# A hybrid decoder block on one core: gates reloaded for eight V chunks at a time, seven activation slots fewer, and one input load handed from SyncE to GpSimd

## The chip, the cores and the metric

The kernel runs on one core of one Trainium2 chip. The metric is the device time of one launch in microseconds (us). Three runs of the kernel before gave 1536.69, 1538.11 and 1542.17 us; the median is 1538.11 us. Differences of about half a per cent (some 8 us) are what such runs can tell from no change.

## The reference

One layer of a decoder over 512 tokens of 1024 numbers: a mixer (16 SSD heads and 8 latent-attention heads, one output projection), a layer norm, a PEER expert mixer, a layer norm. The change touches only the PEER part:

```
def peer(x, w_query, sub_keys, u_table, v_table):
    def block(xb):                                   # blocks of 128 tokens
        q = (xb @ w_query).reshape(T, 8, 2, 128)
        s = einsum('thkd,hknd->thkn', q, sub_keys)
        ...                                          # top 16 of each half, top 16 of the 256 sums
        gate = softmax(top_s)                        # 8 heads x 16 experts for each token
        u = take(u_table, expert_idx)                # 16384 experts, rows of 1024
        act = gelu(einsum('td,thkd->thk', xb, u))
        v = take(v_table, expert_idx)
        return einsum('thk,thkd->td', gate * act, v)
```

## The kernel before

Tokens 0 to 383 of the PEER part are worked densely and the last 128 sparsely. The dense way multiplies all 16384 experts: the u table stands in 128 chunks of 128 experts (`ut`), each a tile of 128x1024, and so does the v table. A "U chunk" is 24 matmuls of 304 columns (three passes of a split into a high and a low part, written `wih` and `wil`), then Gelu into an activation tile (`act`, `acts`). A "V chunk" multiplies the activations of 128 experts by their gates (`P`), splits the product (`Ph`, `Pl`) and adds 18 matmuls of 512 columns into six accumulators (`va`). Tokens 304 to 383 (80 sets) get their u products row by row instead (`urow`: 80 gathers by GpSimd, each followed by one VectorE product), and tokens 384 to 511 are wholly sparse: 128 gathered u rows and 128 gathered v rows (`row`).

The stages in order of time, in the profiled execution: mixer and norms to about 410 us; queries and top-16 to 528 us; decoding of the indices to about 605 us; the build of the gates from 605 to about 840 us; the V stage from 866 us to the end. U chunks are worked beside queries, decoding and build, 88 of them (`PRE`) ahead of the V stage. In the build, 48 steps each make the gates of eight tokens by one-hot products on VectorE, copies on ScalarE and matmuls on TensorE; finished gates of 32 tokens (a block) are scaled into activations that already exist (`late`, L1332, for the first `done[k]` chunks) and the gates of the other chunks are stored to memory (`gsp`). In the V stage they come back chunk by chunk into `gt`. The first 20 V chunks (`GAP`) go alone, then the last 40 U chunks and V chunks alternate ("pairs"), then V chunks go alone again.

What orders the work: one instruction stream for each engine, written out when the program is built. SyncE's queue issues the loads of `ut` and `v` (L113), each into one of four raw tiles, once the split that read the old content is done. In the build, a running sum of estimated times (`tm`) for TensorE and VectorE decides where the halves of a U chunk are put; whether such a half falls into a stretch marked `beside` decides whether GpSimd (L143, 2.4 us) or VectorE (L145, 1.2 us) makes the low part. The u gathers of the 80 sets run six rows ahead (`UROWS`), each issued when a row is used up.

Activations live in `LEAD = KEEP + MORE + REST` slots (47 + 12 + 8 = 67). U chunks beyond the slots that are open are stored (`asp`) and fetched back by GpSimd (`refill`, L1433) as V chunks free slots; `GAP = PRE - LEAD - 1` follows from it.

At 528 us the input rows of the sets are loaded into unused columns of `XT`: two loads and one by GpSimd (L1538, L1539), and eight of 16 partitions each by SyncE (L1541, tile `UR["xb"]`, pieces of 256 B), for the last 16 sets.

Of the kernel before, what the change touches and what calls it, by code (L numbers as in the profile page):

```python
# [11 lines left out]
F32 = mybir.dt.float32  # L12
# [6 lines left out]
OP = mybir.AluOpType  # L19
# [22 lines left out]
REST = 8  # L42
# [10 lines left out]
GP = 4  # L53
# [18 lines left out]
def tile_block(ctx: ExitStack, tc: tile.TileContext, I, out):  # L72
# [1080 lines left out]
    def ug_dots():  # L1153
# [3 lines left out]
        for n in range(UG):  # L1157
            r = UR.pop(n)
            V.scalar_tensor_tensor(r, r, 1.0, UR["xp"], op0=OP.mult, op1=OP.mult,  # L1159
                                   accum_out=hd[:, n:n + 1] if n < UA else hb[:, n - UA:n - UA + 1])  # L1160
            ug_fetch(n + UROWS)
            if n == 1:
                G.dma_start(UR["ixb"], bass.AP(tensor=ixd.tensor, offset=ixd.offset, ap=[[UB, 128 // UB], [128, UB], [1, UB]]))
            if n == UA + 3:
                w = UR["w"]
                A.activation(hd[UA:], hd[UA:], AF.Gelu)
                nc.scalar.dma_start(w[:UA, UA:], hd[UA:])
                A.activation(w[:UA, :UA], hd[:UA], AF.Gelu)
            yield 1.2
            if n == UA - 1:  # L1170
                for e in range(2):
                    A.activation(wide(UR["xp"][:, e * 512:(e + 1) * 512]), UR["xb"][:, e * 8:(e + 1) * 8], AF.Copy)
                yield 0.1
# [67 lines left out]
    def build_g():  # L1241
# [44 lines left out]
        for n in range(48):  # L1286
# [27 lines left out]
            if g % 4 == 3:  # L1314
                k = n // 4
                if k < ND:
                    done.append(min(FIRST, un[0] // 4 * 4))
# [222 lines left out]
    for i in range(0, 128, UB):  # L1540
        nc.sync.dma_start(UR["xb"][i:i + UB], wide(xsp[2, UA - UB:UA]))  # L1541
# [89 lines left out]
    def load_g(q):  # L1631
        if 2 <= q < 32 and q not in gt:
            gt[q] = vst.tile([128, NT // 32, 4, 32], F32, name="gt", bufs=2)
            nb = open_(q * 4)
# [8 lines left out]
    def step_g():  # L1643
        if more_g:
            q, b0, b1 = more_g.pop(0)
            m = min(b1, b0 + GP)
            nc.sync.dma_start(gt[q][:, b0:m], gsp[b0:m, :, q * 4:q * 4 + 4, :].rearrange("b j i t -> j b i t"))
# [5 lines left out]
    for q in range(2):  # L1653
        load_g(q)
    while more_g:
        step_g()
# [14 lines left out]
    def v_prep(c):  # L1671
        load_g(c // 4)
        if c % 4 == 0:
            load_g(c // 4 + 1)
# [4 lines left out]
        if nb:  # L1679
            V.tensor_tensor(P[:, :nb * 32].rearrange("p (b t) -> p b t", t=32), a[:, :nb * 32].rearrange("p (b t) -> p b t", t=32),  # L1680
                            gt[c // 4][:, :nb, c % 4, :], op=OP.mult)
        if nb < ND:
            A.activation(P[:, nb * 32:NU], a[:, nb * 32:], AF.Copy)
        A.activation(P[:, NU:].rearrange("p (b t) -> p b t", t=32), G0[:, :, c] if c < 8 else gt[c // 4][:, ND:, c % 4, :], AF.Copy)
        if c > 8 and c % 4 == 3:
            gt.pop(c // 4)
# [3 lines left out]
    def v_sb(c, nm):  # L1690
        if c > LASTC:
# [237 lines left out]
```

## Time and profile before

| quantity | value |
|---|---|
| median of 3 runs | 1538.11 us |
| profiled execution | 1536.83 us |
| its span | 1535.1 us |
| TensorE (PE) busy | 1503.5 us, 98% |
| VectorE (DVE) busy | 1352.3 us, 88% |
| ScalarE (ACT) busy | 769.3 us, 50% |
| GpSimd (POOL) busy | 719.3 us, 47% |
| memory traffic over the span | 428.27 MB, 279 GB/s |

The profiled execution lies 1.3 us under the median and 1.7 us over its own span. TensorE's busy share is an average over stages; what matters is where its few idle microseconds lie, what ended them, and where the granted clock falls below full speed (1.00 is 2.4 GHz, 0.50 is 1.2 GHz).

### The profile page before, as it was taken

The numbers are of one execution on the slowest core, as the hardware profiler recorded it, in microseconds if no ns is written. First come the engines' busy times: TensorE is split into PE (matmuls) and PEld (weight loads), VectorE is DVE, ScalarE is ACT, GpSimd is POOL, SyncE is SP. The second block draws the span as 40 slices with busy tenths as digits, with TensorE's granted clock in tenths as the row PEclk, the third lists the DMA queues.
The fourth block names the chain that finished last, engine by engine and source line by source line (L and its number), as shares of the span: only waits on it lengthen the run. The fifth ranks groups of instructions, "written<-read, shape, count | busy, mean of one in ns | idle before, by whom it ended". The sixth has DMA issues, their size and how long they took to land.

```text
span 1535.1 us, 24872 instructions
## 1 busy us (share of the span) xinstructions
PE 1503.5 (98%) x8664; PEld 1317.7 (86%) x8664; DVE 1352.3 (88%) x2672; ACT 769.3 (50%) x1541; POOL 719.3 (47%) x522
## 2 busy tenths in 40 slices
PE   9999999999999989999999999999999999999997
PEld 7787888878888989998898988999998888888886
DVE  8979768745799989999899588999999999999998
ACT  5564477742333445775666554444444344443442
POOL 0010032420144532778762477666657676776530
PEclk9999999999999999999999999999999999999999
DMA  7243122375423576999998999999999999999994
GB/s 259 94 149 104 57 71 60 110 248 164 141 76 90 141 243 196 388 398 392 404 381 296 357 400 388 395 382 404 400 399 398 397 395 385 381 388 383 372 318 151
DMA packets 159118, 428.27 MB, mean 279 GB/s; under 512 B 18056, under 2 KB 59984, under 8 KB 158736
## 3 DMA queue, kind: packets, MB, share of 16 engines
q1 hardware_dynamic: 98336, 211.72, 39.7%
q0 software_dynamic: 55104, 196.65, 33.6%
q10 hardware_dynamic: 5552, 18.31, 3.1%
q8 instruction: 68, 1.11, 0.3%
q14 instruction: 58, 0.48, 0.1%
HBM read 393.37 MB, written 31.08 MB: 277 GB/s over the span
## 4 chain that ended last, share of the span: by engine, by line
PE 64%; DVE 18%; DMA 8%; issue 4%; ACT 3%; POOL 2%; DVEq 0%; ACTq 0%; POOLq 0%; SPq 0%
PE va L1721 9%; PE va L1724 9%; PE va L1720 9%; PE pu L90 6%; PE pu L91 6%; PE pu L92 5%; DMA wir<-ut 3%; PE pa L91 3%; PE pa L92 3%; PE pa L90 3%; DVE wil L145 2%; DMA row<-v,ix 2%; DVE t L1033 1%; PE pw L90 1%; PE pw L92 1%
## 5 line engine op out<-in xcount | busy, mean ns | idle before, releaser
L131 ACT ACTIVATE wih<-wir 128x1024 fp32r<-128x1024 f32 (+2 forms) x269 | 277.2, 1032 | 159.3 <-DMA wir<-ut 54.0
L145 DVE TENSOR_TENSOR wil<-wir,wih 128x1024 fp32r<-128x1024 f32 (+1 forms) x212 | 255.8, 1208 | 54.1 <-ACT wih L131 41.6
L92 PE MATMUL pu<-XT,wil 128*128 128x304 f32 x1000 | 300.8, 301 | 0.0
L1721 PE MATMUL va<-wil,Ph 128*128 128x512 f32 x726 | 283.1, 390 | 2.8 <-DVE wil L145 2.8
L1586 POOL DMA_INDIRECT row<-v,ix x128 | 222.0, 1734 | 97.4 <-DVE ac L1607 76.8
L90 PE MATMUL pu<-XT,wih 128*128 128x304 f32 x824 | 251.3, 305 | 6.6 <-ACT acts L1449 4.9
L91 PE MATMUL pu<-XT,wih 128*128 128x304 f32 x824 | 250.6, 304 | 0.0
L1586 POOL DMA_INDIRECT row<-u,ix x128 | 180.1, 1407 | 132.4 <-DVE row L1601 67.6
L92 PEld LDWEIGHTS pu<-XT,wil 128*128 128x128 f32 x1000 | 189.4, 189 | 0.0
L1720 PE MATMUL va<-wih,Ph 128*128 128x512 f32 x486 | 189.1, 389 | 0.0
L1607 DVE SCALAR_TENSOR_TENSOR ac<-row,hd,ac 128x1024 f32<-128x1024 f32 x128 | 164.1, 1282 | 4.5 <-DMA row<-v,ix 2.9
L1601 DVE SCALAR_TENSOR_TENSOR row<-row,XT 128x1024 f32<-128x1024 f32 x128 | 154.5, 1222 | 15.1 <-DMA row<-u,ix 14.4
L90 PEld LDWEIGHTS pu<-XT,wih 128*128 128x128 f32 x824 | 156.3, 190 | 9.4 <-ACT acts L1449 5.3
L1721 PEld LDWEIGHTS va<-wil,Ph 128*128 128x128 f32 x726 | 136.3, 188 | 31.4 <-DVE wil L145 4.5
L91 PEld LDWEIGHTS pu<-XT,wih 128*128 128x128 f32 x824 | 156.8, 190 | 1.6
L1724 PE MATMUL va<-wih,Pl 128*128 128x512 f32 x486 | 149.9, 390 | 0.4 <-DVE Pl L1711 0.3
L145 POOL TENSOR_TENSOR wil<-wir,wih 128x1024 fp32r<-128x1024 f32 (+3 forms) x37 | 77.9, 2113 | 145.1 <-ACT wih L131 121.4
L1703 ACT ACTIVATE Ph<-P 128x384 fp32r<-128x384 f32 x121 | 63.1, 522 | 156.0 <-DVE P L1680 132.9
L1724 PEld LDWEIGHTS va<-wih,Pl 128*128 128x128 f32 x486 | 91.1, 188 | 20.0 <-DVE Pl L1711 1.3
L1720 PEld LDWEIGHTS va<-wih,Ph 128*128 128x128 f32 x486 | 91.2, 188 | 18.1
L1159 DVE SCALAR_TENSOR_TENSOR urow<-urow,xp 128x1024 f32<-128x1024 f32 x80 | 93.8, 1215 | 4.0 <-DMA urow<-u,uix 1.8
L1150 POOL DMA_INDIRECT urow<-u,uix x64 | 81.9, 1280 | 30.1 <-DVE urow L1159 13.3
(527 smaller groups left out, 3484.8 us busy)
## 6 DMA issues: line engine op xcount, KB each, us to landing
wir<-ut SPq DMA_DIRECT2D x128, 512.0 KB
wir<-v SPq DMA_DIRECT2D x86, 512.0 KB
wirx<-v SPq DMA_DIRECT2D x42, 512.0 KB
gt<-gsp SPq DMA_DIRECT2D x63, 256.0 KB
wir<-wo SPq DMA_DIRECT2D x26, 512.0 KB
gsp<-stg ACTq DMA_DIRECT2D x24, 448.0 KB
wir<-wf SPq DMA_DIRECT2D x18, 512.0 KB
wir<-wqr SPq DMA_DIRECT2D x16, 512.0 KB
```

The source lines that it names most:

```text
L90: T.matmul(ps, lh, rh, start=start, stop=False)
L91: T.matmul(ps, lh, rl, start=False, stop=False)
L92: T.matmul(ps, ll, rh, start=False, stop=stop)
L131: A.activation(h, r, AF.Copy)
L145: self.lo(n).tensor_tensor(l, r, h, op=OP.subtract)
L1159: V.scalar_tensor_tensor(r, r, 1.0, UR["xp"], op0=OP.mult, op1=OP.mult, accum_out=hd[:, n:n + 1] if n < UA else hb[:, n - UA:n - UA + 1])
L1586: G.indirect_dma_start(out=R[s], out_offset=None, in_=I["u"] if s < 128 else I["v"], in_offset=bass.IndirectOffsetOnAxis(ap=ix3[:, s % 128 ...
L1601: V.scalar_tensor_tensor(wide(r), wide(r), 1.0, x3, op0=OP.mult, op1=OP.mult, accum_out=hd[:, s:s + 1])
L1607: V.scalar_tensor_tensor(ac, r, hd[:, s - 128:s - 127], ac, op0=OP.mult, op1=OP.add)
L1720: T.matmul(va[b][e], Ph[b], h[:, cs], start=c == 0, stop=False)
L1721: T.matmul(va[b][e], Ph[b], l[:, cs], start=False, stop=False)
L1724: T.matmul(va[b][e], Pl[b], h[:, cs], start=False, stop=c == 127)
```

## The change

Four things change. The stored gates are reloaded for eight V chunks at a time (`GC = 8`) in pieces of 8 x 32 numbers (1 KB) instead of 4 x 32 (512 B), two blocks to a load instead of four, so a load still has 256 KB; the two `gt` tiles double in size. `REST` goes from 8 to 1, so there are 60 activation slots and `GAP` becomes 27. The eight `xb` loads leave SyncE's queue at 528 us and are issued by GpSimd among the gathers of sets 2 to 9, in the early build. The `done` counts are rounded down to multiples of 8 (32, 32 and eight times 40 instead of 32, 36 and eight times 44), and three of the seven last V chunks (121 to 123) keep their split products in the ordinary tiles instead of freed activation slots.

```
-REST = 8
+REST = 1
...
-GP = 4
+GP = 2
+GC = 8
...
             if n == 1:
                 G.dma_start(UR["ixb"], bass.AP(tensor=ixd.tensor, offset=ixd.offset, ap=[[UB, 128 // UB], [128, UB], [1, UB]]))
+            if 1 < n < 2 + 128 // UB:
+                G.dma_start(UR["xb"][(n - 2) * UB:(n - 1) * UB], wide(xsp[2, UA - UB:UA]))
...
-                    done.append(min(FIRST, un[0] // 4 * 4))
+                    done.append(min(FIRST, un[0]) // GC * GC)
...
-    for i in range(0, 128, UB):
-        nc.sync.dma_start(UR["xb"][i:i + UB], wide(xsp[2, UA - UB:UA]))
...
-        if 2 <= q < 32 and q not in gt:
-            gt[q] = vst.tile([128, NT // 32, 4, 32], F32, name="gt", bufs=2)
-            nb = open_(q * 4)
+        if 0 < q < 128 // GC and q not in gt:
+            gt[q] = vst.tile([128, NT // 32, GC, 32], F32, name="gt", bufs=2)
+            nb = open_(q * GC + GC - 1)
...
-            nc.sync.dma_start(gt[q][:, b0:m], gsp[b0:m, :, q * 4:q * 4 + 4, :].rearrange("b j i t -> j b i t"))
+            nc.sync.dma_start(gt[q][:, b0:m], gsp[b0:m, :, q * GC:q * GC + GC, :].rearrange("b j i t -> j b i t"))
...
-        load_g(c // 4)
-        if c % 4 == 0:
-            load_g(c // 4 + 1)
+        if c % GC == 0:
+            load_g(c // GC + 1)
...
-        if c > LASTC:
+        if c > LASTC + 3:
```

SyncE's queue at the end of the queries (528 us). `wir` are raw weight tiles, `XT` the columns that take the sets' inputs, `iaE` a constant for the decoding. Before:

```order
L113 DMA wir<-wqr 128x1024
L113 DMA wir<-ut 128x1024 x10
L1541 DMA XT<-xsp 16x16x64 x8
L1549 DMA iaE<-ch 128x256
L113 DMA wir<-ut 128x1024 x40
```

and now (line numbers are one to three higher):

```order
L114 DMA wir<-wqr 128x1024
L114 DMA wir<-ut 128x1024 x10
L1550 DMA iaE<-ch 128x256
L114 DMA wir<-ut 128x1024 x40
L1458 DMA asp<-aout 128x320
```

The eight loads are gone from between the tenth and the eleventh `ut` tile; nothing else stands between them but one small load.

VectorE in the build, from the scaling of the fourth finished block on (`urow` are set products, `oj`, `g` the one-hot factors, the MEMSET of one column goes with a low part that GpSimd makes). Before:

```order
L1332 TENSOR_TENSOR acts<-acts,stg 128x44x32
L142 MEMSET wil 128x1
L1159 SCALAR_TENSOR_TENSOR urow,uhd<-urow,xp 128x1024 x2
L1264 TENSOR_TENSOR oj<-iotaE,jT 128x1024
L1270 TENSOR_TENSOR g<-tens,units 128x2048
L142 MEMSET wil 128x1
L1159 SCALAR_TENSOR_TENSOR urow,uhd<-urow,xp 128x1024 x3
L145 TENSOR_TENSOR wil<-wir,wih 128x1024
```

and now:

```order
L1335 TENSOR_TENSOR acts<-acts,stg 128x40x32
L1160 SCALAR_TENSOR_TENSOR urow,uhd<-urow,xp 128x1024 x2
L146 TENSOR_TENSOR wil<-wir,wih 128x1024 x2
L1267 TENSOR_TENSOR oj<-iotaE,jT 128x1024
L1273 TENSOR_TENSOR g<-tens,units 128x2048
L143 MEMSET wil 128x1
L1160 SCALAR_TENSOR_TENSOR urow,uhd<-urow,xp 128x1024 x3
L1267 TENSOR_TENSOR oj<-iotaE,jT 128x1024
```

The scaled block is four chunks smaller, and VectorE makes two low parts in a stretch where it made one and GpSimd two. Over the whole program GpSimd makes 22 low parts instead of 26 at L143, and VectorE four more.

SyncE's queue among the pairs, where all 12 blocks of gates come back. Before:

```order
L1647 DMA gt<-gsp 128x4x128
L113 DMA wirx<-v 128x1024
L113 DMA wir<-ut 128x1024
L1647 DMA gt<-gsp 128x4x128
L113 DMA wir<-v 128x1024
L113 DMA wir<-ut 128x1024
L1647 DMA gt<-gsp 128x4x128
```

and now:

```order
L1648 DMA gt<-gsp 128x2x256
L114 DMA wir<-v 128x1024
L114 DMA wir<-ut 128x1024
L1648 DMA gt<-gsp 128x2x256
L114 DMA wir<-v 128x1024
L114 DMA wirx<-ut 128x1024
L114 DMA wir<-v 128x1024
```

Loads of the same size come at six of eight V chunks instead of three of four; the fourth raw tile (`wirx`) now takes u chunks among the pairs, where it took v chunks.

## Rows read from the trace of the kernel before

**Rows 1.** Stretches: us, busy PE, PEld, DVE, ACT, POOL, PEclk, DMA share, GB/s.
```profile
530.00:560.00 30.00, 25.75 (x175) 25.50 (x175) 27.00 (x35) 14.88 (x28) 4.60 (x6) 0.94 0.76 180
600.00:650.00 50.00, 49.34 (x439) 48.41 (x438) 49.27 (x75) 33.28 (x82) 35.59 (x26) 1.00 0.91 342
...
750.00:800.00 50.00, 47.67 (x386) 45.42 (x385) 47.10 (x77) 34.76 (x86) 36.76 (x24) 0.97 1.03 397
...
1150.00:1200.00 50.00, 49.03 (x273) 43.47 (x272) 48.27 (x57) 21.61 (x42) 37.39 (x23) 1.00 1.04 397
1200.00:1250.00 50.00, 47.87 (x264) 41.92 (x263) 47.77 (x49) 18.67 (x38) 35.91 (x23) 1.00 1.03 399
...
1300.00:1350.00 50.00, 50.00 (x222) 41.39 (x221) 49.32 (x59) 21.01 (x38) 37.38 (x20) 1.00 1.04 380
```

**Rows 2.** Waits between 500 and 560 us: us in total, times, longest.
```profile
ACT wih L131 <- DMA wir<-ut: 5.5, 1, 5.5
...
PE pu L90 <- ACT acts L1449: 4.3, 1, 4.3
```

**Rows 3.** SyncE's queue in order of time, 505 to 620 us: start, us.
```profile
527.94 5.20 SPq L1541 DMA_DIRECT2D XT<-xsp  x8
...
536.12 83.22 SPq L113 DMA_DIRECT2D wir<-ut  x25
```

**Rows 4.** Chain that ended last, 522 to 560 us: start, us, what.
```profile
536.12 6.64 DMA wir<-ut
...
542.84 1.06 ACT wih L131
```

**Rows 5.** Busy time around the wait of rows 2; columns as in rows 1.
```profile
541.00:546.00 5.00, 0.74 (x5) 0.50 (x4) 2.94 (x2) 3.13 (x6) 0.00 (x0) 0.98 0.60 236
546.00:549.00 3.00, 3.00 (x13) 3.00 (x13) 2.52 (x2) 2.72 (x6) 0.00 (x0) 0.50 0.61 175
```

**Rows 6.** VectorE's waits, 530 to 620 us.
```profile
DVE wil L145 <- ACT wih L131: 2.8, 2, 1.6
DVE eq L1106 <- ACT tif L1098: 1.3, 1, 1.3
```

**Rows 7.** Groups of instructions (count, busy us, mean ns, idle before).
```profile
L145 DVE TENSOR_TENSOR wil<-wir,wih 128x1024 fp32r<-128x1024 f32 (+1 forms) x212 | 255.8, 1208 | 54.1 <-ACT wih L131 41.6
L1159 DVE SCALAR_TENSOR_TENSOR urow<-urow,xp 128x1024 f32<-128x1024 f32 x80 | 93.8, 1215 | 4.0 <-DMA urow<-u,uix 1.8
L1332 DVE TENSOR_TENSOR acts<-acts,stg 128x1408 f32<-128x1408 f32 (+2 forms) x10 | 15.6, 1564 | 0.0
L143 POOL TENSOR_TENSOR wil<-wir,wih 128x1024 fp32r<-128x1024 f32 x20 | 48.3, 2413 | 22.9 <-DVE wil L142 14.7 <-ACT wih L131 3.7 <-DVE urow L1159 2.1
```

**Rows 8.** VectorE's waits in the build, 605 to 850 us.
```profile
DVE wil L145 <- ACT wih L131: 2.6, 1, 2.6
...
DVE urow L1159 <- DMA urow<-u,uix: 1.8, 1, 1.8
```

**Rows 9.** GpSimd in order of time, 515 to 640 us.
```profile
525.13 2.40 POOL L145 TENSOR_TENSOR wil<-wir,wih 128x1024 fp32r<-128x1024 f32 x1 [0.90 <-PE pu L92]
...
554.33 0.54 POOL L1137 DMA_DIRECT2D uix<-p  x1 [18.76 <-DVE uix L1138]
...
569.43 3.04 POOL L1150 DMA_INDIRECT urow<-u,uix  x1 [0.30 <-issue]
```

**Rows 10.** DMA queues (packets, MB, share of 16 engines), and one group of issues.
```profile
q1 hardware_dynamic: 98336, 211.72, 39.7%
q0 software_dynamic: 55104, 196.65, 33.6%
...
gt<-gsp SPq DMA_DIRECT2D x63, 256.0 KB
```

**Rows 11.** TensorE's wait and VectorE's, 1140 to 1260 us.
```profile
PE va L1721 <- DVE wil L145: 2.8, 3, 1.4
...
DVE ac L1607 <- DMA row<-v,ix: 2.9, 4, 1.4
```

More of the change, by code (lines that the diff above doesn't have):

```diff
@@ L1651, in step_g @@
                 step_g()
[L1653 to L1656, printed above, removed]
     next(fill)
@@ L1680, in v_prep @@
             V.tensor_tensor(P[:, :nb * 32].rearrange("p (b t) -> p b t", t=32), a[:, :nb * 32].rearrange("p (b t) -> p b t", t=32),
-                            gt[c // 4][:, :nb, c % 4, :], op=OP.mult)
+                            gt[c // GC][:, :nb, c % GC, :], op=OP.mult)
         if nb < ND:
             A.activation(P[:, nb * 32:NU], a[:, nb * 32:], AF.Copy)
-        A.activation(P[:, NU:].rearrange("p (b t) -> p b t", t=32), G0[:, :, c] if c < 8 else gt[c // 4][:, ND:, c % 4, :], AF.Copy)
-        if c > 8 and c % 4 == 3:
-            gt.pop(c // 4)
+        A.activation(P[:, NU:].rearrange("p (b t) -> p b t", t=32), G0[:, :, c] if c < GC else gt[c // GC][:, ND:, c % GC, :], AF.Copy)
+        if c > GC and c % GC == GC - 1:
+            gt.pop(c // GC)
         prepared[0] += 1
```

## The prediction

> **What bounds the kernel now.** I read the busy time by stretch first. TensorE is idle for 31.6 us of a span of 1535.1 us, and most of that lies in few places [rows 1]: 4.25 us between 530 and 560, 0.7 to 2.3 us in each 50 us of the build, 3.1 us between 1150 and 1250. Elsewhere in the V stage it is busy for 50.00 of 50 us. VectorE is busy for 49.27 of 50 us at the start of the build and 47.10 near its end, so there VectorE, not TensorE, sets the pace; in the last V chunks it has 0.7 of 50 us to spare, with TensorE full. A change to the reloads of the V stage can therefore win back little more than 3.1 us; the larger prize is the stop at 541 us.
>
> The waits of that stretch say what it is [rows 2]: TensorE waited 4.3 us for ScalarE to empty a U chunk's sum, and ScalarE had waited 5.5 us for a `ut` tile to land. The chain shows it in order [rows 4]: tile issued at 536.12, landed 6.64 us later, copied by ScalarE from 542.84, the emptying behind it. Why it was issued so late stands in SyncE's queue [rows 3]: from 527.94 the eight `xb` loads take 5.20 us to issue, and the next `ut` load comes at 536.12, 8.2 us after the first of them. The raw tile that it fills had been free since about 527.5, when GpSimd's split ended (525.13 + 2.40) [rows 9]. The granted clock then stands at 0.50 from 546 to 549 us, after an interval with only 0.74 us of work in 5 [rows 5].
>
> **The change part by part.**
>
> *The `xb` loads leave SyncE.* The `ut` load can go at 527.9 + 0.4 for the small constant, 528.3. Even if it again takes 6.64 us it lands at 535.0, and ScalarE is ready for it at 542.84 - 5.5 = 537.3. The stop should vanish: TensorE regains 4.26 us and, at half clock for 3 us, half of that, 1.5; together 5.8 us. VectorE regains less. It stood idle for 2.8 us behind ScalarE's copies and 1.3 us behind another ScalarE step [rows 6], 4.1 us. Since the build behind it goes at VectorE's pace, I take **-4.1**; bounds 0 (another wait takes its place) and -5.8 (TensorE's gain goes through).
>
> *The same loads on GpSimd in the early build.* The smallest direct load there took 0.54 us to issue and a gather up to 3.04 [rows 9]. Eight at 0.54 are 4.3 us, spread over eight sets. Behind them on GpSimd stand the gathers and the low parts. The gathers run six rows ahead, and the 80 sets [rows 7] share the 235 us from 605 to 840, 2.9 us each on average: 17 us of cover for a delay that grows to 4.3. Over the whole build GpSimd is also relieved of four low parts of 2.41 us [rows 7]. I take **0**; bounds 0 and the 24 - 17 = +7 us of eight loads at 3.04.
>
> *VectorE in the build.* Four low parts come over from GpSimd: 4 x 1.208 = 4.8 us, less four small MEMSETs (0.2). The scaling of finished blocks shrinks by 4 chunks nine times: the ten take 15.6 us for 32 + 36 + 8 x 44 = 420 chunk columns, 0.037 each, so 36 fewer are -1.3 us [rows 7]. Net +3.3 us of work on the engine that sets the pace. Not all is felt: in the build VectorE still waits for copies (2.6 us) and a gathered row (1.8 us) [rows 8], and work put ahead of such a wait is free. I take half, **+1.7**; bounds 0 and +3.3. If the waits are gone, it is 3.3.
>
> *The U chunks stand elsewhere in the build.* They are as many as before, but come up to one and a half chunks earlier in the middle and leave less for the last three steps. Nothing in the trace prices it; stops there cost 0.7 to 2.3 us per 50 us, and a mean granted clock of 0.97 over 50 us [rows 1] is 1.5 us more: **0**, bounds -4 and +4 (one such stop less, or one more).
>
> *Gates in larger pieces, and the longer pairs.* The stop between 1150 and 1250 us is VectorE late with a low part, itself behind gathered v rows [rows 11], with the DMA engines' share at 1.03 to 1.04 [rows 1]: too many bytes for the time of a pair. It falls where pairs meet chunks that need all 12 blocks (from chunk 44 on): 16 pairs before (44 to 59), 23 now (44 to 66). 3.1 us x 23 / 16 = 4.5, so +1.4. Against it, what a 512 B piece costs. SyncE's queue moved 211.72 MB in 39.7% of 16 engines' span, GpSimd's 196.65 MB in 33.6% [rows 10]. Were all of SyncE's other bytes moved at GpSimd's 23.8 bytes per ns, the 63 large gate loads (16.5 MB) would be left with 1559 us of engine time, 97 us of all sixteen; at the same 23.8 they need 43. Twice the piece at the price of one piece saves half of 97, 49 us over the V stage; at the price of its bytes, nothing. A chunk with all 12 blocks (0.197 MB, 1/84 of it) saves 0 to 0.58 us. I take a quarter, since a queue at nearly full rate leaves the gates little excess, and SyncE's larger packets also carry some of it: 0.14 us x 23 pairs = 3.2 us less demand, about as much as the stop is worth. But rows and splits are issued in a fixed order, and a stop shrinks by less than the demand does; I let it pay for the longer pairs: **0**, bounds -3.1 (no stop left) and +1.4. The rule of the Trainium skill that bears on this (DMA: Bandwidth & Descriptors, Specifications) gives 512 B as the size from which a transfer reaches line rate; by it the pieces were large enough already, and the sum would be 1.4 us higher. The trace's bound of 0 allows that.
>
> *Seven slots fewer.* Seven of 41 fetches move from the start of the V stage to V chunks 20 to 26, one to a chunk as in the first 20. Those chunks are worked alone, TensorE has no stop there, and GpSimd, at 37 of 50 us in its busiest stretches [rows 1], has room: **0**. The first load for chunks 8 to 15 is now asked for when chunk 0 is prepared, and each last part three chunks ahead instead of two: a gain in time for loads that are not waited for by TensorE, **0**.
>
> *The last seven chunks.* Three of them use the ordinary split tiles again, which come free when TensorE is done three chunks earlier. That is how all 121 chunks before them work: **0**.
>
> **Sum.** -4.1 + 1.7 = -2.4 us. The profiled execution's own 1536.83 becomes 1534.4. It lay 1.3 us under the median, so against the median of 1538.11 I predict **1535.7 us**, 0.16% faster. That is less than the 0.5% (7.7 us) that a measurement of this kernel can tell from no change.
>
> **Rivals.**
>
> *TensorE's whole gain comes through (faster).* 5.8 at 541 us, no exposed VectorE work, and no stop among the pairs (3.1): 8.9 us, 1529.2. For it: U chunks after 541 are fed by loads, and all of them come earlier. Against it: VectorE's 49.27 of 50 us.
>
> *The longer pairs fall behind (slower).* Place: V chunks 44 to 66. The 16 full pairs cost 0.19 us each now, after 24 lighter pairs in which rows could run ahead; there are now only 17 lighter ones. If rows come late in earnest, at 0.5 us a pair, 23 pairs cost 11.5 instead of 3.1, +8.4, and two falls of the clock at 1.5 add 3: 1535.7 + 11.4 = 1547. It decides from 0.45 us a pair on. For it: VectorE's waits for rows and a DMA share over 1. Against it: the row plan per unit of work is the same and the gates ask for no more bytes.
>
> *Larger pieces change nothing.* The gates cost by the byte, as the skill's rule above has it, the longer pairs are paid in full: 1535.7 + 1.4 = 1537.1.
>
> *GpSimd is held up by VectorE.* If each of the eight loads takes what the slowest gather took, 3.04 us [rows 9], the rows of sets 8 to 15 come up to 24 - 17 = 7 us beyond their cover, VectorE stands still for them, and TensorE's clock falls once: 1535.7 + 7 + 1.5 = 1544. For it: the gathers in the decoding did take 3. Against: the small direct loads beside them took 0.54. The Trainium skill (SBUF — State Buffer, SBUF: two separate sides) says that a DMA issued from GpSimd cannot have its descriptors written while VectorE runs an operation in a two-port mode; that speaks for this rival.
>
> **How the numbers follow.** The likeliest case 0.56 (by itself 1530 to 1541, the bounds of the build's order and VectorE's work), faster rival 0.14, longer pairs 0.13, pieces without effect 0.09, GpSimd held up 0.08. Faster by over 0.5% is under 1530.4: most of the faster rival, 0.12. Slower by over 0.5% is above 1545.8: two thirds of the longer pairs, a third of the held-up case, and a little of the build's order, 0.14. The rest, 0.74, is the same. The range is 1529 to 1544: it leaves out half of the faster rival and most of the slower one.
>
> **What would show it.** In the new trace: no wait of ScalarE for `wir<-ut` near 537 us, and no stretch at 0.50 at 546; eight loads of about 0.6 us on GpSimd between the gathers around 610 us, and no VectorE wait for `urow` there; VectorE's busy time in the build up by 3 us; TensorE idle for 2 to 5 us between 1100 and 1270. Wrong would be: a stop of TensorE over 3 us in the build that was not there, VectorE waiting for `urow` by more than 5 us, or TensorE idle for over 8 us among the pairs.

## The result and the profile after

The changed kernel took 1550.9 us (median of 6 runs, 1547.49 to 1555.30) beside 1538.87 us for the kernel before on the same chip: 1.008 times the time, 95% interval 1.006 to 1.0099. Measured again: 1.0078, 1.0062 to 1.0094. That is 12 us slower; 2.4 us faster was forecast, and the range ended at 1544. The profiled execution took 1547.49 us, with a span of 1545.7.

**Where the time went.** Stretches of the changed kernel, columns as in [rows 1]:

```profile
530.00:560.00 30.00, 30.00 (x217) 29.66 (x217) 29.56 (x37) 16.93 (x33) 6.85 (x7) 1.00 0.65 178
560.00:600.00 40.00, 37.36 (x259) 36.87 (x258) 35.59 (x42) 19.30 (x41) 10.96 (x6) 0.96 0.65 228
600.00:650.00 50.00, 44.54 (x364) 42.72 (x363) 43.05 (x64) 27.43 (x67) 36.44 (x32) 0.93 0.94 322
640.00:646.00 6.00, 5.02 (x26) 4.16 (x26) 5.96 (x9) 5.65 (x16) 1.65 (x1) 0.50 1.02 362
850.00:900.00 50.00, 46.91 (x319) 41.98 (x317) 33.23 (x42) 29.07 (x64) 19.17 (x19) 1.00 0.97 352
...
1150.00:1200.00 50.00, 48.47 (x271) 42.92 (x271) 47.51 (x64) 21.12 (x42) 31.20 (x24) 1.00 1.03 403
1200.00:1250.00 50.00, 48.99 (x274) 43.31 (x273) 48.68 (x51) 20.03 (x37) 32.49 (x23) 1.00 1.03 404
1250.00:1300.00 50.00, 48.08 (x253) 41.42 (x252) 48.84 (x52) 19.73 (x38) 34.08 (x23) 1.00 1.03 398
```

The stop at 541 us is gone, as forecast: TensorE is busy for 30.00 of 30 us where it had 25.75 [rows 1]. But it then stands for 2.64 us between 560 and 600, and for 5.46 us between 600 and 650, where it had 0.66; behind that stop it runs at 1.2 GHz (0.50) from 640 to 646. At the start of the V stage (850 to 900) 3.09 us are lost that were not lost before. Among the pairs, between 1150 and 1300 us, 4.46 us are lost; before, it was 3.1 up to 1250 [rows 1] and 0.15 in the 50 behind.

The waits between 560 and 650 us (us in total, times, longest):

```profile
ACT wih L132 <- DMA wir<-ut: 27.4, 8, 10.4
...
PE pw L1312 <- ACT g L1277: 3.8, 1, 3.8
...
PE pu L91 <- ACT acts L1452: 3.3, 2, 2.3
...
DVE urow L1160 <- DMA urow<-u,uix: 2.6, 3, 1.7
```

ScalarE waits for one `ut` tile for 10.4 us, and TensorE at last for ScalarE, which has a gate factor (`g`) queued behind that copy. VectorE waits 2.6 us for gathered rows, where it waited for none between 600 and 650 us before. SyncE's queue shows why the tile is late; of the changed kernel:

```profile
618.88 0.33 SPq L114 DMA_DIRECT2D wir<-ut  x1
...
633.90 0.33 SPq L114 DMA_DIRECT2D wir<-ut  x1
```

and of the kernel before:

```profile
619.01 0.33 SPq L113 DMA_DIRECT2D wir<-ut  x1
...
625.33 0.33 SPq L113 DMA_DIRECT2D wir<-ut  x1
...
630.38 1.54 SPq L113 DMA_DIRECT2D wir<-ut  x2
```

Fifteen microseconds pass without a load, where there were 6.3. What GpSimd and then VectorE did meanwhile, in the changed kernel:

```profile
624.26 0.62 POOL L1166 DMA_DIRECT2D XT<-xsp  x1
624.90 2.42 POOL L144 TENSOR_TENSOR wil<-wir,wihx 128x1024 fp32r<-128x1024 f32 x1
...
630.39 2.39 POOL L144 TENSOR_TENSOR wil<-wir,wih 128x1024 fp32r<-128x1024 f32 x1
...
630.28 3.59 DVE L146 TENSOR_TENSOR wil<-wir,wih 128x1024 fp32r<-128x1024 f32 x1
```

and the last of these low parts of GpSimd in the kernel before:

```profile
627.96 2.39 POOL L143 TENSOR_TENSOR wil<-wir,wih 128x1024 fp32r<-128x1024 f32 x1
```

The eight loads took what was forecast, 0.62 us each, but GpSimd's low parts are some 2 us later, and VectorE's split, which takes 1.21 us alone [rows 7], takes 3.59 beside one. The next `ut` load is issued 0.03 us after that split. The first reading was that GpSimd's queue did this. It was wrong, as the runs below show.

The start of the V stage, from the chain that ended last:

```profile
864.62 9.16 DMA gsp<-stg
...
873.88 0.47 ACT P L1679
...
875.10 0.50 PE va L1716
```

ScalarE's first product `P` waits until a store of the last gates has landed. Before, ScalarE had no such wait there.

VectorE's low parts rose by 3 in [rows 7]'s group (by 4 over all shapes, 263 to 267), and SyncE's queue sent fewer packets than in [rows 10]:

```profile
L146 DVE TENSOR_TENSOR wil<-wir,wih 128x1024 fp32r<-128x1024 f32 (+1 forms) x215 | 261.8, 1219 | 65.3 <-ACT wih L132 42.7
...
q1 hardware_dynamic: 79072, 211.78, 38.9%
```

The packets fell by a fifth. The share times the span fell from 609 to 601 us of all sixteen engines, 8 us, where 1 KB pieces at the price of 512 B would have saved 49. (Where the text ahead says that a `ut` load goes into one of four raw tiles: that holds for the V stage; in the build there are three.)

### The profile page after: what moved, and what is told of

The parts are those of the page before. It is cut to its first block, busy times and chain, and to the rows that moved or that the text cites. A ratio compares the mean times of both kernels' runs of the same rounds, so it can differ in the third digit from the quotient of the medians.

```text
span 1545.7 us, 24820 instructions
## 1 busy us (share of the span) xinstructions
PE 1505.3 (97%) x8664; PEld 1317.3 (85%) x8664; DVE 1354.1 (88%) x2669; ACT 766.3 (50%) x1534; POOL 691.9 (45%) x526
## 5 line engine op out<-in xcount | busy, mean ns | idle before, releaser
L146 DVE TENSOR_TENSOR wil<-wir,wih 128x1024 fp32r<-128x1024 f32 (+1 forms) x215 | 261.8, 1219 | 65.3 <-ACT wih L132 42.7
L1587 POOL DMA_INDIRECT row<-v,ix x128 | 213.0, 1664 | 100.4 <-DVE ac L1608 75.4
L1716 PE MATMUL va<-wih,Ph 128*128 128x512 f32 x606 | 236.0, 389 | 2.1 <-ACT Ph L1699 2.1
L1587 POOL DMA_INDIRECT row<-u,ix x128 | 170.1, 1329 | 146.7 <-DVE row L1602 91.9
L91 PE MATMUL pu<-XT,wih 128*128 128x304 f32 x664 | 202.9, 306 | 4.3 <-ACT acts L1452 3.3
L92 PE MATMUL pu<-XT,wih 128*128 128x304 f32 x664 | 201.3, 303 | 0.0
L1720 PE MATMUL va<-wih,Pl 128*128 128x512 f32 x606 | 186.6, 389 | 0.0
L1716 PEld LDWEIGHTS va<-wih,Ph 128*128 128x128 f32 x606 | 113.8, 188 | 24.1 <-ACT Ph L1699 2.3
L1720 PEld LDWEIGHTS va<-wih,Pl 128*128 128x128 f32 x606 | 113.8, 188 | 23.7
L91 PEld LDWEIGHTS pu<-XT,wih 128*128 128x128 f32 x664 | 125.7, 189 | 6.5 <-ACT acts L1452 4.1
L92 PEld LDWEIGHTS pu<-XT,wih 128*128 128x128 f32 x664 | 125.9, 190 | 0.8
L91 PE MATMUL pu<-XT,wihx 128*128 128x304 f32 x336 | 102.3, 304 | 4.1 <-ACT aout L1456 4.1
L92 PE MATMUL pu<-XT,wihx 128*128 128x304 f32 x336 | 101.9, 303 | 0.0
```

Source lines behind the costliest of these rows:

```text
L91: T.matmul(ps, lh, rh, start=start, stop=False)
L92: T.matmul(ps, lh, rl, start=False, stop=False)
L146: self.lo(n).tensor_tensor(l, r, h, op=OP.subtract)
L1587: G.indirect_dma_start(out=R[s], out_offset=None, in_=I["u"] if s < 128 else I["v"], in_offset=bass.IndirectOffsetOnAxis(ap=ix3[:, s % 128 ...
L1716: T.matmul(va[b][e], Ph[b], h[:, cs], start=c == 0, stop=False)
L1720: T.matmul(va[b][e], Pl[b], h[:, cs], start=False, stop=c == 127)
```

## The experiments

Times are ratios to the kernel before on the same chip, from 6 to 12 runs against 17 to 29, with 95% intervals; 0.001 is 1.54 us. The quotient of the two medians differs from the ratio given by up to 0.0011, so differences of one or two thousandths between runs are weak evidence.

### One part undone, or one part alone

The loads back on SyncE at 528 us:

```
-            if 1 < n < 2 + 128 // UB:
-                G.dma_start(UR["xb"][(n - 2) * UB:(n - 1) * UB], wide(xsp[2, UA - UB:UA]))
...
+    for i in range(0, 128, UB):
+        nc.sync.dma_start(UR["xb"][i:i + UB], wide(xsp[2, UA - UB:UA]))
```

> The changed kernel with the eight xb loads back on SyncE at 528 us; everything else as changed. Theory A (the loads on GpSimd make its low part late, VectorE's split collides with it, the next ut load comes 2 to 8 us late, TensorE stops at 636 us and runs at half clock behind it): the stop at 636 us (3.8 + 0.7 + 1.0 us idle, two intervals at half clock) is gone, the stop of 4.3 us at 541 us is back, u chunk 42 starts 6 to 7 us earlier than in the changed kernel, the whole is 6.6 us faster than it, 1544 us, 1.0035 of before. Rival B (the stop comes from the other order of U chunks and low parts or from chance): the stop at 636 us stays, the stop at 541 us is added, 1551 to 1555 us. The wait at the start of the V stage (873 us) stays under both.

**1.0035 (1.0022 to 1.0047).** As theory A had it: no stop between 600 and 650 us, the stop at 541 back (3.90 us). So the move costs some 7 us here. Columns as in [rows 1]:

```profile
530.00:560.00 30.00, 26.10 (x179) 25.85 (x178) 27.72 (x34) 15.10 (x29) 5.35 (x6) 0.94 0.73 178
600.00:650.00 50.00, 49.95 (x440) 48.72 (x440) 49.34 (x75) 33.95 (x83) 36.35 (x26) 1.00 0.93 347
```

The first gates asked for one chunk later, so that `P` gets its old address:

```
-        if c % GC == 0:
+        if c % GC == 0 and c or c == 1:
             load_g(c // GC + 1)
```

> The changed kernel, but the first tile of gates is asked for when V chunk 1 is prepared instead of chunk 0, so that P, Ph and Pl get the addresses they had before and gt lies behind them. Theory A (P of V chunk 0 lies on the last bytes of a staging tile of the build, and ScalarE waits 3.6 us until the last store from it has landed): the wait of ScalarE's P for gsp<-stg is gone, TensorE's 2.1 us stop at 873 us too, V chunk 0 starts 3 to 5 us earlier, the whole is 1546 to 1548 us, 1.005 to 1.006 of before. Rival B (the V stage starts late because VectorE is late with the last build steps and fewer U chunks are left): V chunk 0 starts within 1 us of where it did, the whole 1550 to 1551 us. Rival C (the store is merely the last in a chain that other work hides): the wait goes but the V chunks wait for the v tiles that SyncE issues at the same time, 1549 to 1551 us.

**1.0054 (1.0031 to 1.0078).** The ratio fits theory A, the profile does not (waits between 858 and 880 us):

```profile
ACT P L1679 <- DMA gsp<-stg: 2.9, 1, 2.9
```

`P` has its old address and still waits for the store. The theory of P's address fell, and a ratio whose interval touches that of the changed kernel does not save it.

The move alone, on the kernel before (the same two edits the other way round):

> The kernel before with only the move of the eight xb loads to GpSimd, among the gathers of sets 2 to 9. Theory A: the stop at 541 us goes, but TensorE meets the burst of gathers at 568 us and is 1 us ahead at 600 us; between 620 and 645 us it stops as in the changed kernel (4 to 6 us idle, two intervals at half clock), u chunk 42 starts 6 to 7 us later than before, the whole is 1544 to 1547 us, 1.0035 to 1.005 of before. Rival B (the loads on GpSimd are harmless, the build's loss has another cause): 1533 to 1536 us, 0.996 to 0.998.

**1.0012 (1.0000 to 1.0025).** The stop came as in the changed kernel:

```profile
600.00:650.00 50.00, 44.37 (x352) 42.12 (x352) 44.45 (x63) 28.54 (x68) 38.33 (x32) 0.93 0.96 320
```

The price did not: 2 us, between the ranges of theory A and rival B. What the move gains at 541 us is in it too.

Seven slots fewer alone (`REST = 1`, and `c > LASTC + 3` in `v_sb`):

> The kernel before with only REST = 1 (seven slots fewer, 27 V chunks alone before the pairs) and, as that needs, three of the last seven V chunks in ordinary tiles. Theory A: build and start of the V stage as before; the V stage is longer by 0 to 2 us for the seven longer pairs with all blocks, 1539 to 1541 us, 1.000 to 1.0015. Rival D (fewer slots or longer pairs are where the loss of the V stage lies): TensorE stops among the pairs by 3 us more than before, 1542 us or more.

**1.0016 (1.0005 to 1.0027).** 2.5 us, just above theory A's range. From 900 us to 1526 TensorE lost 5.56 us, where the kernel before lost 3.25; but a second profile of the kernel before (below) lost 5.36 in that stretch, so the profiles don't show where the 2.5 us lie.

### The same loads by SyncE, and what is left

The eight loads at the same sets, but issued by SyncE, on the kernel before:

```
+            if 1 < n < 2 + 128 // UB:
+                nc.sync.dma_start(UR["xb"][(n - 2) * UB:(n - 1) * UB], wide(xsp[2, UA - UB:UA]))
```

> The kernel before; the eight xb loads are issued by SyncE, not at 528 us but among its ut loads, beside the gathers of sets 2 to 9 (about 600 to 620 us). Theory A (what costs is GpSimd's queue, not the moment): the stop at 541 us goes, the stop between 620 and 645 us that the loads on GpSimd bring does not come; the lead of TensorE at 600 us (1 to 3 us, what the burst of gathers at 568 us leaves of it) stays; 0.997 to 0.999 of before, 2 to 5 us under the run with the loads on GpSimd alone. Rival E (eight small loads in the early build delay the ut loads wherever they are issued, through the DMA engines or 0.65 us of issue each): a stop between 605 and 645 us as with GpSimd, 1.001 of before or more.

**1.0031 (1.0016 to 1.0046).** Rival E. ScalarE waits 8.6 us for one tile (waits between 600 and 646 us):

```profile
ACT wih L131 <- DMA wir<-ut: 10.2, 3, 8.6
```

SyncE's queue and ScalarE's copy show what was late:

```profile
621.84 0.33 SPq L113 DMA_DIRECT2D wir<-ut  x1
622.22 1.38 SPq L1165 DMA_DIRECT2D XT<-xsp  x1
626.90 10.28 SPq L113 DMA_DIRECT2D wir<-ut  x3
...
634.45 1.06 ACT L131 ACTIVATE wih<-wir 128x1024 fp32r<-128x1024 f32 x1 [8.55 <-DMA wir<-ut]
```

and the copy of the tile that the kernel before asks for at 625.33:

```profile
633.27 1.06 ACT L131 ACTIVATE wih<-wir 128x1024 fp32r<-128x1024 f32 x1 [3.88 <-DMA wir<-ut]
```

The raw tiles rotate as before. The small load takes 1.38 us of the queue, but the late tile had been asked for ahead of it, at 621.84, and is copied 12.6 us later, against 7.9 in the kernel before; the `ut` load behind the small one is issued 3.3 us after that one's end. So it is the landing that is late here, not the issue; why is not shown.

The same in the changed kernel, with the gates one chunk later:

> The changed kernel with two things mended: the xb loads by SyncE among its ut loads beside sets 2 to 9, and the first tile of gates asked for at V chunk 1, so that P has its old address. Theory A, by the ratios measured so far: changed kernel 1.008, less 0.0045 to 0.006 for the loads off GpSimd's queue and 0.0026 for P, 0.9995 to 1.001 of before. Rival (what is left of the change, the order of U chunks and the gates, costs too): 1.003 or more.

**1.0068 (1.0047 to 1.0088)**, the rival; its stop at 636 us is 7.65 us long, with the raw tiles in unbroken rotation too. Among the loads of the early build SyncE's queue is no better place.

The loads back at 528 us and the gates one chunk later (the first two edits together):

> The changed kernel with the xb loads back on SyncE at 528 us and the first tile of gates asked for at V chunk 1: what is left of the change is the gates in 1 KB pieces, the counts rounded to eight, and seven slots fewer. If the costs of the loads and of P add up: 1.008 - 0.0045 - 0.0026 = 1.001 of before. The seven slots alone gave 1.0016, so the larger pieces and the rounding would then be worth between -0.001 and 0. Rival F (the two costs are not separate, and the stop of one hides in the other): 1.003 or more.

**1.0056 (1.0040 to 1.0073).** Rival F: no better than the loads alone put back (1.0035), so the edit on the gates is worth nothing that these runs can tell.

> The kernel before once more, for a second profile of it: how far its stops in the build (0.7 to 2.3 us in each 50 us) lie at other places in another execution. If they do, differences of 2 us in the build can't be read from one profile. Stops at 541 and 1150 to 1250 us are expected in both; the time 1535 to 1543 us.

1541.88 us, span 1540.1. The stop at 541 us was there (25.18 of 30 us busy), and the build's stops lay within 1.5 us of where they were, two (0.66 and 0.72 us) gone and two (0.63 us at 698 and 1.41 us at 721) new. Between 1140 and 1250 us TensorE lost 4.96 us, where the first profile has 3.1 between 1150 and 1250 [rows 1]:

```profile
1140.00:1200.00 60.00, 57.06 (x320) 50.48 (x320) 55.49 (x71) 24.69 (x48) 37.36 (x27) 1.00 1.03 392
1200.00:1250.00 50.00, 47.98 (x268) 42.18 (x267) 48.26 (x50) 21.27 (x41) 29.33 (x23) 1.00 1.03 397
```

So two microseconds among the pairs can't be read from one profile.

### Moment, order and gates apart

On the kernel before, the loads by GpSimd at 528 us:

```
     G.dma_start(UR["x3"], wide(xsp[3]))
+    for i in range(0, 128, UB):
+        G.dma_start(UR["xb"][i:i + UB], wide(xsp[2, UA - UB:UA]))
```

> The kernel before; the eight xb loads leave SyncE and are issued by GpSimd at 528 us, right behind the other input loads, so that no load is left in the early build. The stop of 4 us at 541 us should go. Theory E (eight small loads in the early build cost, by whichever engine): no stop between 628 and 645 us, TensorE keeps a lead of 1 to 3 us, 0.997 to 0.999 of before. Theory G (with the stop at 541 us gone the engines stand in another phase to each other, and VectorE's split then meets GpSimd's without any load beside it): the stop of 3 to 5 us at 630 to 645 us is there all the same, 1.001 to 1.003 of before.

**0.9985 (0.9972 to 0.9997).** Theory E, so far: no stop in the early build, and faster than both kernels.

```profile
530.00:560.00 30.00, 27.92 (x202) 27.63 (x201) 29.23 (x36) 15.94 (x31) 10.16 (x15) 1.00 0.78 189
...
600.00:650.00 50.00, 49.94 (x440) 48.71 (x439) 49.28 (x78) 34.84 (x85) 37.77 (x28) 1.00 0.94 354
```

On the kernel before, only the rounding, which gives the build the changed kernel's order:

```
-                    done.append(min(FIRST, un[0] // 4 * 4))
+                    done.append(min(FIRST, un[0]) // 8 * 8)
```

> The kernel before with only the done counts rounded down to eight, which gives the U chunks, the low parts and the scalings of the build the order of the changed kernel (xb loads at 528 us, slots and gates as before). Theory H (the order is part of the loss: the U chunks run out at step 45 of 48, and the low parts move to VectorE): stops at 860 and 872 us of about 1 us each, more idle time between 740 and 830 us, 1.002 to 1.004 of before. Rival (the order costs nothing, as predicted; the loss lies in the gates' larger tiles and loads): 0.999 to 1.001.

**1.0016 (1.0000 to 1.0032)**, between theory H's range and the rival's, and only just clear of no change. The profile is theory H's in part: TensorE lost 6.6 us between 740 and 830, where the two profiles of the kernel before lost 4.0 and 3.8, and 1.02 us between 850 and 900, the stop at 857; the one at 872 did not come.

The changed kernel, loads at 528 us on SyncE, gates one chunk later, and the running sum charged as before:

```
-                lump += 0.15 + done[k] * 0.034
+                lump += 0.15 + (32, 36, 44)[min(k, 2)] * 0.034
```

> The changed kernel with the xb loads at 528 us, the first gates asked for at V chunk 1, and the running sum charged as before, so that the build's order is that of before; what is left of the change: gates of eight chunks in 1 KB pieces, smaller scalings, seven slots fewer. Theory H: no stops at 860 and 872 us; 1.0016 (the seven slots) with the larger pieces worth nothing, 0.9995 to 1.001 with a gain from them. Rival (the larger tiles and loads cost): 1.003 or more, as the same kernel had with the changed order (1.0056).

**1.0030 (1.0018 to 1.0043)**, the rival's lower end. `P` still waits 2.9 us for the last store here, and TensorE loses 1.41 us by it, so this is not the price of the larger loads alone. Without the old order it was 1.0056, so the order is 4 us by this pair and 2.5 by the run of the rounding alone.

> The changed kernel once more, on the chip of the other three, for its ratio there and a second profile. 1.006 to 1.010 of before; the stops at 568, 636, 718 and 873 us are expected again, with sizes that may differ by 1 to 3 us.

**1.0078 (1.0062 to 1.0094)**, with the four stops at 568, 635, 718 and 875 us (2.02, 3.93, 2.40 and 1.23 us).

### The raw tile, and the pool

Runs with the stop at 636 us on GpSimd had one thing in common that the order of the instructions doesn't show. Here are the three raw tiles of the build, by address, in the order of the loads from 33 to 46, in the programs as built:

```
kernel before, loads at 528 us, loads by SyncE:  b a c b a c b a c b a c b a
changed kernel, move alone, gates later:         b a c b a c c b c a b c a b
```

and what the 38th to 41st load wait for, kernel before and changed kernel:

```
153 L113 DMA wir_6555<-ut 128x1024 [waits DMAHW3_49,Pool_49]
154 L113 DMA wir_6631<-ut 128x1024 [waits DMAHW4_49,Pool_49]
155 L113 DMA wir_6697<-ut 128x1024 [waits DMAHW5_49,Pool_49]
156 L113 DMA wir_6739<-ut 128x1024 [waits DMAHW6_49,DVE_49]
...
148 L114 DMA wir_6551<-ut 128x1024 [waits DMAHW3_49,Pool_49]
149 L114 DMA wir_6630<-ut 128x1024 [waits DMAHW7_49,DVE_49]
150 L114 DMA wir_6697<-ut 128x1024 [waits DMAHW4_49,Pool_49]
151 L114 DMA wir_6739<-ut 128x1024 [waits DMAHW1_49,DVE_49]
```

Load 39 is given tile c, into which load 38 has just gone, while b, free at 627.32 (624.90 + 2.42), waits for a load that stands behind it. It can't start until load 38 has landed, been copied by ScalarE and split by VectorE, which was at 633.87. Which tile a load gets is settled when the program is built; eight more instructions on GpSimd were enough to turn it. Three names in place of one rotating name forbid it, with every engine's order unchanged:

```
-                    t = self.p.tile(self.shape, F32, name=self.name + "r", bufs=3)
+                    t = self.p.tile(self.shape, F32, name=self.name + "r" + "abc"[self.nr % 3], bufs=1)
+                    self.nr += 1
```

> The changed kernel, every engine's instructions in the same order; only the three raw tiles are given to the loads in fixed rotation. In the changed kernel one ut load of the early build (the 39th load of that list) gets the tile of the load just ahead of it again, so that it waits for that load to land and for VectorE's split of it, with the other two tiles empty; in the kernel before, and where the loads are at 528 us, the rotation is unbroken. Theory T (this one tile is the stop at 636 us, and the eight loads on GpSimd cost next to nothing themselves): SyncE's ut load that came at 633.9 us comes at 623 to 626 us, the stop at 636 us and the two half-clock intervals go, u chunk 36 starts 6 to 9 us earlier, the whole is 1.0035 to 1.0055 of before (4 to 7 us under the changed kernel, as later waits take some of it back). Rival A (GpSimd's queue, its low part and the collision with VectorE): the stop stays at 2 us or more, 1.007 to 1.008.

**1.0040 (1.0028 to 1.0052)**: theory T. The eight loads stand where they stood, and VectorE's split beside GpSimd's still takes long, but the `ut` loads come; in order of time:

```profile
625.22 0.33 SPq L116 DMA_DIRECT2D wirc<-ut  x1
...
629.11 2.36 POOL L146 TENSOR_TENSOR wil<-wira,wih 128x1024 fp32r<-128x1024 f32 x1
...
629.64 2.92 DVE L148 TENSOR_TENSOR wil<-wirb,wih 128x1024 fp32r<-128x1024 f32 x1
...
631.50 0.33 SPq L116 DMA_DIRECT2D wira<-ut  x1
632.59 0.33 SPq L116 DMA_DIRECT2D wirb<-ut  x1
```

and the stretch, columns as in [rows 1]:

```profile
600.00:650.00 50.00, 47.12 (x406) 44.72 (x405) 48.12 (x69) 31.73 (x78) 40.21 (x33) 1.00 0.96 333
```

The clock stays at 1.00. Of the stops 1.02 us are left at 636.65, and 1.72 at 629.81, where TensorE waits for GpSimd's low part: that much of theory A holds. With 47.12 of 50 us against 49.95 where the loads were put back, and 1.0040 against 1.0035 in time, the move brings nothing here even with the rotation mended.

The gate tiles in a pool of their own, order unchanged:

```
     vst = pool("vst")
+    gtp = pool("gtp")
...
-            gt[q] = vst.tile(
+            gt[q] = gtp.tile(
```

> The changed kernel, every engine's instructions in the same order; only the two gate tiles get a pool of their own behind the one of P, Ph and Pl. In the changed kernel that pool reaches 3 KB into the last staging tile of the build, since it holds the gate tiles too, and its first writer, ScalarE's P of V chunk 0, waits for all that used its space, the last gate store included. Theory (the pool's extent, not P's own address, makes the wait): P no longer waits for gsp<-stg (3.6 and 2.8 us), TensorE's stop of 1.2 to 2.1 us at 873 us goes, V chunk 0 starts 2 to 4 us earlier, 1.0055 to 1.0065 of before. Rival (another wait stands behind it: the v tiles whose raw tile lies on the same staging tile): the wait moves to a v tile, V chunk 1 or 2 stops instead, 1.007 to 1.009.

**1.0069 (1.0053 to 1.0085)**, between the two ranges; the profile is the rival's. The wait of `P` is gone, so the pool's extent was its cause; but the `v` tiles are late instead (880 to 892 us), and TensorE stops at 888 for 1.64 us:

```profile
ACT wih L132 <- DMA wir<-v: 6.6, 2, 4.3
...
PE va L1717 <- ACT Ph L1700: 1.6, 1, 1.6
```

The changed kernel with all three mended (loads by GpSimd at 528 us, own pool, old sum):

> The changed kernel with three things mended: the xb loads by GpSimd at 528 us behind the other input loads, the gate tiles in a pool of their own, and the running sum charged as before so that the build's order is the old one. What is left of the change: gates of eight chunks in 1 KB pieces, seven slots fewer. By the ratios so far: 0.9985 for the loads, +0.0016 for the slots, between 0 and +0.0014 for the gates: 1.000 to 1.0015 of before, 10 us under the changed kernel. If another cost of the change is still hidden, 1.003 or more.

**1.0016 (1.0004 to 1.0029).** And the kernel before with loads by GpSimd at 528 us and seven slots fewer:

> The kernel before with the xb loads by GpSimd at 528 us and seven slots fewer, gates as before (four chunks, 512 B pieces): 0.9985 + 0.0016 = 1.000 of before. Beside it, the mended kernel shows what the larger pieces alone are worth: a gain would put it below this one by up to 3 us (0.002), the price of a transfer by bytes at the same time within 0.001, and a cost of the larger tiles above it.

**1.0002 (0.9993 to 1.0011).** The second as expected, the first just above its range. In this last run TensorE still loses 4.44 us between 530 and 560, as much as the kernel before (4.25). The larger pieces (with the smaller scalings and the own pool) are worth +0.0014, 2 us the wrong way, with some 0.0015 of uncertainty on either side: not clear of nothing.

### What the move can bring

The loads by GpSimd behind the first set (583 us), fixed rotation, on the kernel before:

```
+            if n == 0:
+                for i in range(0, 128, UB):
+                    G.dma_start(UR["xb"][i:i + UB], wide(xsp[2, UA - UB:UA]))
```

> The kernel before with the xb loads on GpSimd behind the gather that follows the first set (about 583 us), where GpSimd has nothing else until the build, and the raw tiles in fixed rotation; other engines' instructions in the old order. If the two costs found are all that the move can cost (the tile handed out twice, and the loads between GpSimd's low parts or in SyncE's queue): the stop at 541 us goes, no stop at 630 to 645 us, TensorE 2 to 4 us ahead at 600 us; 0.997 to 0.9985 of before, as good as or 1 us better than the loads at 528 us on GpSimd (0.9985). If the small loads themselves disturb the build through the DMA engines, wherever they are: 1.000 or more.

**0.9994 (0.9981 to 1.0008)**, short of what was expected: the stop at 541 us is gone, but TensorE stands 1.87 us at 568 and has 37.20 of 40 us from 560 on. And four of the first six gathers held back by an addition on GpSimd that reads the next indices:

```
-        for n in range(UROWS):
+        for n in range(2):
             ug_fetch(n)
...
+            if b == 1:
+                pace = p.tile([128, 2], F32, name="pace")
+                G.tensor_tensor(pace, IJG[1][:, 0, 0, :2], IJG[1][:, 0, 0, 2:4], op=OP.add)
+                for n in range(2, UROWS):
+                    ug_fetch(n)
```

> The same kernel, with four of the six gathers that are issued together at 557 to 570 us held back until the next group of indices is decoded (about 577 us). In all runs without the stop at 541 us TensorE then stood 1.1 to 2.4 us at 568 to 571 us, ScalarE waiting for ut tiles while the gathers land. If that burst takes back part of the gain: the stop at 568 us goes or falls under 0.5 us, TensorE is 1 to 3 us further ahead at 600 us than without the change, 0.996 to 0.9975 of before. If VectorE sets the pace of the decoding, the lead is gone again by 600 us and the time is that of the run without it within 1 us; if the held-back rows come late for the build, VectorE waits for urow and the time is 2 us or more above it.

**0.9967 (0.9956 to 0.9977)**, 1535.09 us: the fastest of all, some 4 us under the run without it and 5 under the kernel before. The stop at 568 is gone and the clock no longer falls in the decoding. The stretch in the run without the edit:

```profile
560.00:600.00 40.00, 37.20 (x253) 36.17 (x252) 34.44 (x42) 19.16 (x41) 15.49 (x13) 0.96 0.73 238
```

and with it:

```profile
560.00:600.00 40.00, 37.21 (x263) 35.99 (x262) 36.41 (x42) 18.96 (x41) 13.42 (x14) 1.00 0.81 251
```

A new stop of 1.63 us stands at 593 us, so TensorE's busy time is the same, but at the full clock it does 263 matmuls in it instead of 253, and VectorE does 2 us more work. Which of the two sets the pace from here on is not shown.

## Why the prediction was wrong

**The stop at 541 us (-4.1): right in kind, wrong in room and size.** One reading under it was wrong. The load at 536.12 did not fill the tile that GpSimd freed at 527.53; the load of 527.56 took that one. Its own tile came free behind VectorE's split (532.20 + 1.22). In the kernel before:

```profile
527.56 0.33 SPq L113 DMA_DIRECT2D wir<-ut  x1
...
532.20 1.22 DVE L145 TENSOR_TENSOR wil<-wir,wih 128x1024 fp32r<-128x1024 f32 x1
```

and in the changed kernel:

```profile
527.64 0.43 SPq L1550 DMA_DIRECT2D iaE<-ch  x1
...
531.91 1.22 DVE L146 TENSOR_TENSOR wil<-wir,wih 128x1024 fp32r<-128x1024 f32 x1
...
533.16 0.33 SPq L114 DMA_DIRECT2D wir<-ut  x1
```

So the load came 3 us earlier, not 8, and ScalarE still waited 1.20 us for it (copy at 538.23), where the sum saw 2.3 us of room (535.0 against 537.3). The stop at 541 went in every run that took the eight loads out of SyncE's queue there, but 2.1 to 4.0 us of it stayed, at 545, where GpSimd issues them at 528. Elsewhere TensorE, earlier by 5 us, runs into the gathers at 557 to 570 us and stops there for 1.5 to 2.4 us. Counted from the trace, U chunk 24 is emptied 1.3 us earlier in the changed kernel and 3.5 in its second profile. The run with the loads at 583 us has the gain without the other costs: 0.9994, 1 us, which its interval does not tell from nothing. Holding the gathers back brings some 4 us more. The gain was there, and the next wait took most of it; the bound of 0 was given for that, the value was not.

**The same loads on GpSimd (0): the step that failed.** The term was put at nothing because a delay of 4.3 us would stay under 17 us of cover. The time of a load was right (0.62 us); the cover was not, since VectorE waited 2.6 us for gathered rows; and the greater cost lay where the prediction did not look: load 39 got the tile of load 38, and the `ut` stream stood for 15.0 us instead of 6.3. The fixed rotation gives back 0.0038, 6 us (1.0078 to 1.0040). In the kernel before, the move with the same broken rotation is at 1.0012 and the loads at 528 us are at 0.9985, 4 us apart. The rival that GpSimd is held up by VectorE did not come: 0.62 us, not 3.04. The section that spoke for it, SBUF: two separate sides of the Trainium skill (SBUF — State Buffer), also says that of a VectorE operation on two tensors in SBUF and a GpSimd operation that reads SBUF one waits until the other is done. The trace agrees with that: the split of 3.59 us ended at 633.87, 1.09 us behind GpSimd's low part (630.39 + 2.39), and alone it takes 1.21.

**The order of the U chunks (0, bounds -4 and +4) and VectorE's work (+1.7): inside the bounds.** The rounding brings both, and the runs measure them together: 2.5 us by the rounding alone (interval 0 to 4.9), 4 us by the pair of runs with the sum mended, against 1.7 in the sum. The U chunks end a step earlier, and TensorE waits at 857 to 863 us for a gate factor (1.01 to 1.02 us in each profile with this order). VectorE's busy time over the program rose by 1.8 us (1352.3 to 1354.1), not 3.3.

**The longer pairs (+1.4): right in kind, 2.5 us.** The slots alone cost 0.0016, and again 0.0017 (0.9985 to 1.0002) on the kernel with the loads at 528 us. The rival of 8.4 us did not come. The edits counted at nothing beside it (fetches later, three of the last chunks in ordinary tiles) are in these 2.5 us and not told apart.

**The larger pieces (a gain of 1.4, to pay for the pairs): no gain.** +2.2 us, the same in two pairs of runs (1.0030 against 1.0016, 1.0016 against 1.0002), each uncertain by some 2.5 us, and the first of them with the wait of `P` in it. The rival of pieces that change nothing was the nearer one, and the rule that it had from the Trainium skill (DMA: Bandwidth & Descriptors, Specifications: line rate from 512 B on) agrees: twice that size bought no time. SyncE's queue did spend a lower share on the same bytes, but no wait became shorter by it that the profiles show: between 1140 and 1300 us TensorE lost 6.85 us with the larger pieces and 4.38 without, in the last pair of runs.

**The start of the V stage: not in the prediction.** The gate tiles doubled and took the pool of `P` into the last staging tile (3 KB of it); the first write into the pool waits for all that used its space. Without the wait TensorE stops 15 us later, for the `v` tiles; by the ratios (1.0078 and 1.0069) it is worth 0 to 3 us.

Added up: 6.0 (tile) + 2.5 to 4 (order) + 2.5 (slots) + 2.2 (pieces) - 1 (what the loads gain) is 12.2 to 13.7; measured were 12. Parts that were measured in different surroundings need not add up so well: the two runs that put the loads back differ by 0.0021 although the edit between them leaves the V stage's start, where it bears, as it was (47.82 and 47.70 of 50 us busy from 850 on). What stays open is that difference, what the wait at the V stage's start is worth by itself, and why `ut` tiles land late when SyncE issues the small loads among them. The 6 us of the raw tile are shown by an edit that changes nothing else; the other parts are differences near what the runs can tell.

One more reading is wrong, though no term rests on it: TensorE is not busy for 50 of 50 us everywhere else in the V stage. 8.9 of its 31.6 idle us lie in the last 35 of the kernel before; columns as in [rows 1]:

```profile
1500.00:1535.10 35.10, 26.18 (x116) 21.35 (x114) 28.62 (x67) 8.90 (x19) 2.67 (x5) 0.91 0.38 137
```

## What to carry to other kernels

An instruction that is cheap itself can turn a choice that the program's builder makes elsewhere: after an edit, list the buffers that the critical loads get and what each waits for, before and after, and give a ring that must rotate its own names. A tile that grows in a shared pool makes every first user of the pool wait for what lay under its new end. When a stop is removed, look for what the stop had kept apart: here a burst of six gathers that only now met TensorE's loads.

## What was not expected of the hardware

VectorE's split of 1.21 us took 2.92 to 3.59 us beside a GpSimd operation on two tensors; it was VectorE that waited, by its record the earlier of the two (630.28 and 630.39), and GpSimd's was not slowed (2.39). In both profiles it ended 1.09 us behind GpSimd's operation (633.87 and 632.78, 632.56 and 631.47). Two profiles of one kernel differ by 2 us among the pairs (3.25 and 5.36 us lost between 1140 and 1300).
